# Full 128 rows in the bias product and in the transposes of a mixture-of-experts stage

## The chip, the core and the metric

The kernel runs on one core of one Trainium2 chip. The metric is the device time of one execution in microseconds (us), lower is better. On this kernel a measurement tells apart differences of about 0.2% (some 5 us). The engines are called as in the profile: PE is the tensor engine's products, PEld its loads of the stationary operand, DVE the vector engine, ACT the scalar engine, POOL GpSimd, SP the queue that issues most transfers.

## What is computed

One layer of a decoder on 1024 tokens of 1024 channels, in float32: two token mixers side by side, merged by gates, an output projection and a layer norm; then a mixture of 32 experts, of which each token takes 4, and a second layer norm. The change touches the experts alone. Cut to them, the reference is:

```
logits = (xt @ router_w + router_b); top_vals, top_idx = lax.top_k(logits, 4); gates = softmax(top_vals)
# for every expert e, over the tokens that chose it (xblk):
    hcat = xblk @ w_up[e] + b_up[e]                       # 1024 -> 2048
    x_glu = minimum(hcat[:, 0::2], 7); x_lin = clip(hcat[:, 1::2], -7, 7)
    act = x_glu * sigmoid(1.702 * x_glu) * (x_lin + 1)
    y = act @ w_down[e] + b_down[e]                       # 1024 -> 1024
# out[token] += gate * y
```

## The kernel before

Up to about 1040 us of its span the kernel does the mixers, the projections, the first layer norm and the router. The router writes, for each expert, a list of its tokens to DRAM, and sorts the experts by their counts. The experts then run from about 1045 to 2583 us, and a last layer norm ends the span.

**Two forms of an expert.** `CAPS` gives each place of the sorted order a fixed size n. The 18 largest experts have n from 204 down to 134 and are called *wide*: the weights are the stationary operand and the tokens stream past them. The other 14 have n = 128 and are *narrow*: the tokens are stationary and 512 columns of weights stream past. `SEQ` sets the order in which they run: mostly a wide and a narrow one in turn, and three times two wide ones in a row.

**Precision.** Each float32 operand is split in two parts whose sum it is (`split`: ACT makes the first part, DVE or, for every fifth piece of weights, POOL the second). A product of two split operands takes three products on PE. Weights arrive in transfers of 1 MB into six places (`raw`, `fetch`, issued by SP), are split six pieces of work ahead (`part`) into eight places each for `wh` and `wl`, and are then multiplied.

**Tokens of an expert.** `gather` (an indirect transfer on the POOL queue) brings the expert's tokens as rows into `xg`: block 0 with 128 tokens, and for a wide expert block 1 with the other n - 128, which are 76 for the first expert and 6 for the last wide one. `turn` transposes them on PE by way of the identity `idn`, 128 channels at a time, into a bank of PSUM (`tr`, two buffers), from where `split` makes the two parts in `xTA` (wide) or `xTB` (narrow). A transpose of block 1 works on as many rows as the block has tokens. One call of `turn` handles G channel blocks, as many as fit into 512 columns: 4 of a narrow expert, 3 or 2 of a wide one. So for a wide expert the PE sees an alternation of 128-row and short transposes, in groups of six or four. The groups of the next expert stand between the pieces of the one that runs.

**Biases.** A wide expert adds the bias of its first product while ACT evacuates it. A narrow expert adds it on PE: as the last product into each of its four accumulators (`up_narrow`, L1304), a column of the permutation `perm`, broadcast to 128 columns, is stationary and 512 columns of `bupr` stream past. Both have 64 rows: 32 experts' first parts and, below them, the 32 second parts.

**Order.** Each engine takes its instructions in the order in which the program writes them. `experts` writes it out by hand: a list of pieces (`order`), and beside it a list `side` of small jobs, of which one is called after a piece when nothing else is due. The turns of the next expert are such jobs; those that are left are called just before the next expert's first product.

Of the kernel before, what the change touches and what calls it, by code (L numbers as in the profile page):

```python
# [15 lines left out]
OP = mybir.AluOpType  # L16
# [53 lines left out]
def lockstep(*streams):  # L70
    """Emits generators side by side; each yields the tensor-engine time of the piece it emitted."""
    total = [0.0] * len(streams)
    live = set(range(len(streams)))
    weight = [w for _, w in streams]
    gens = [g for g, _ in streams]
    while live:
        i = min(live, key=lambda j: total[j] / weight[j])
        try:
            total[i] += next(gens[i])
        except StopIteration:  # L80
            live.discard(i)


def shape_constants():
    """Arrays of zeros and ones that hang on the shapes alone."""
# [29 lines left out]
class Block:  # L115
# [56 lines left out]
    def scratch(self):  # L172
        """Expert lists in DRAM: (token, gate) by expert and place; at first every place names a zero row."""
# [16 lines left out]
    def load_x(self):  # L190
        nc, a = self.nc, self.a
        # by half of the tokens
        self.xh = [p.tile([128, KT, 512], F32R, name=f"xh{i}") for i, p in enumerate(self.xpool)]
        self.xl = [p.tile([128, KT, 512], F32R, name=f"xl{i}") for i, p in enumerate(self.xpool)]
        # the place of q and f, which come later, takes the rows
# [21 lines left out]
    def fetch(self, col):  # L217
        """Loads columns col..col+256 of w_in and splits them."""
# [10 lines left out]
    def project(self, jobs, ahead=None):  # L229
        """jobs: (column, halves, evacuate): 256 columns by channel for these halves of the tokens, or by token for  # L230
        all of them where halves is None. A generator over pieces of tensor-engine work.

        ahead: a generator whose steps come before those of the first job.
        """
# [62 lines left out]
    def hgrn_jobs(self):  # L297
        """Projections of the HGRN branch: q^T and f^T by channel, v and the output gate by token."""
# [43 lines left out]
    def hgrn_chunks(self):  # L342
        """Chunks of 128 tokens: one chunk's decays beside the scores of the one before."""
# [17 lines left out]
    def hgrn_front(self, c, state):  # L361
        """Log gates of a chunk, their sums over ranges of tokens, and what these scale."""
# [15 lines left out]
        # q beside what the odd tokens' q keeps of the token before  # L378
# [10 lines left out]
        # decays from each token to the chunk's end  # L389
# [7 lines left out]
        for g, n in enumerate((4, 3)):  # L397
            for h in range(NH):
# [6 lines left out]
                for i in range(n):  # L405
# [5 lines left out]
                    # the first half of each block takes k, the second q  # L411
# [7 lines left out]
    def hgrn_back(self, c, state):  # L419
        """Scores within a chunk, its output, and the state it leaves."""  # L420
# [8 lines left out]
        # a token with itself and with the one before  # L429
# [52 lines left out]
    def rsqrt(self, pool, v, scale, eps, n):  # L482
        """1 / sqrt(v * scale + eps), with a Newton step on the table's value."""
# [14 lines left out]
    def sb_tiles(self):  # L498
        sp = self.spool
        # the first part of a head's keys lies on both halves of the partitions  # L500
        self.kh = sp.tile([128, SBH, T], F32R, name="kh")
        self.kl = sp.tile([128, 4, T], F32R, name="kl")
        self.sv = sp.tile([128, NB, 512], F32, name="sv")

    def sb_jobs(self):
        """q^T, kept in DRAM, k^T in two parts, v by token."""
# [33 lines left out]
    def gates_jobs(self):  # L540
        """The merge gates' arguments, by channel, kept in DRAM until the merge; a part of them early, a part late."""
# [15 lines left out]
    def sb_attention(self):  # L557
        """Weights sigmoid(z_s) * prod over s < s' < t of sigmoid(-z_s'), s < t."""
        nc, wk = self.nc, self.work
        self.os_d = self.dram("osb_scratch", (T, 512))  # L560
        # a unit is a head's block of queries, or several heads' where the keys are few
# [10 lines left out]
        def split_q(i):  # L572
            # the first part on the head's own partitions, the second on the others
# [8 lines left out]
        def heads(u):  # L582
            # those on the same half of the partitions follow one another: their products share a bank
# [4 lines left out]
        def scores(u):  # L588
# [28 lines left out]
            # a token keeps all of what itself and later ones would take  # L617
# [35 lines left out]
        def average(u):  # L653
            # two heads side by side, by channel
# [41 lines left out]
    def turn_branches(self):  # L696
        """The branches' outputs by channel, in two parts."""
# [4 lines left out]
        # the stick-breaking branch is there by channel: its own place in memory takes it  # L702
# [107 lines left out]
    def layer_norm(self, pool, r, st, g, b, out):  # L810
        """From the statistics of both halves of the rows."""
# [9 lines left out]
    def outproj(self):  # L821
# [6 lines left out]
        # the first part of the biases twice and the second, one below the other  # L828
# [3 lines left out]
        def load_biases(i):  # L832
            n = bd.shape[0] if i == 0 else self.bupr.shape[0]
# [5 lines left out]
        def round_biases(i):  # L839
            to = self.bupr[:, D * i - D:D * i] if i else bd  # L840
# [21 lines left out]
        def add(tb, half):  # L862
            """The residual, and the statistics of what results."""
# [5 lines left out]
        def project(tbs):  # L869
            """Blocks of tokens; two at a time follow the loading of the weights row block by row block."""  # L870
# [26 lines left out]
        def route(tb):  # L897
# [10 lines left out]
            # four sums side by side, by expert, then their sum by token  # L908
# [17 lines left out]
            # which experts each token takes, and with what weight  # L926
# [31 lines left out]
            # places within the experts' lists  # L958
# [26 lines left out]
            # what the experts' outputs are added to: the residual and the weighted biases  # L985
# [36 lines left out]
        # then the last block first: the order of the experts waits for it  # L1022
# [11 lines left out]
    def expert_constants(self):  # L1034
        """What the sorting needs, and the biases in two parts, the second below the first."""
# [13 lines left out]
        self.bupr = cp.tile([2 * NE, 2 * D], F32R, name="bupr")  # L1049

    def sort_experts(self):
        """Each expert's place in the order of the counts."""
# [4 lines left out]
        # distinct keys: the count, then the lower expert first  # L1057
# [19 lines left out]
        self.perm = cp.tile([2 * NE, NE], F32R, name="permr")  # L1077
# [3 lines left out]
    def sort_biases(self):  # L1081
        nc, cp = self.nc, self.epool
        # biases of the first product, by channel and place in the order
# [11 lines left out]
    def list_beyond(self):  # L1095
        """What lies beyond the static sizes: blocks of 128 places, listed."""
# [15 lines left out]
        # row of an expert's first block beyond, less 128 for each block listed before  # L1112
# [4 lines left out]
        # one block a partition: its expert and its first row  # L1117
# [15 lines left out]
        # the same along a row  # L1133
# [11 lines left out]
        self.itoh = cp.tile([2 * NE, NITEM], F32R, name="itoh")  # L1145
        nc.vector.tensor_scalar(self.itoh, ps[:2 * NE, :NITEM], self.ecol, None, op0=OP.is_equal)

    # Two forms of an expert's product. Up to 128 places: the tokens are the stationary operand and the
    # weights stream past. More: the weights are stationary and both parts of the tokens stream past them.

    def expert(self, n, e, rows, bias, choice):
# [11 lines left out]
        def gather():  # L1163
            ti = X["ti"]
            xg = wk.tile([128, 2, D], F32, name="xg", bufs=1)
# [6 lines left out]
        G = min(4, 512 // n)  # L1172

        def turn(k0):
# [5 lines left out]
            pv = ps[:, :(k1 - k0) * n].rearrange("p (k n) -> p k n", n=n)  # L1180
            for k in range(k0, k1):
                for i, (s, m) in enumerate(blocks):
                    nc.tensor.transpose(pv[:, k - k0, s:s + m], X["xg"][:m, i, 128 * k:128 * k + 128],
                                        self.idn[:m, :m])
# [567 lines left out]
```

## Time and profile before

| What | Before |
|---|---|
| Device time, median of 3 runs | 2642.2 us (2641.92 to 2643.72) |
| Profiled execution, span from the first to the last instruction | 2635.2 us |
| PE busy over the span | 2507.8 us (95%) |
| DVE, ACT, POOL busy | 1865.8, 1452.9, 866.9 us |
| Experts, first to last product | about 1056 to 2583 us |

The profile is of one execution; its span is 7.0 us shorter than the median time, and this part lies around the span. A busy time is a mean over stages with different limits, so what bounds a stage is read from its own stretch of the trace: from the waits of the engine that is nearly always busy there, and from the starts of its instructions. Products on PE are pipelined and overlap in the trace, so the distance from one start to the next tells their cost, and not the duration.

### The profile page before, as it was taken

Reading aid. Unit: us, or ns where it says so; the run is one execution under the profiler, and the core shown is the slowest. Engines: PE = TensorE matmul, PEld = TensorE weight load, DVE = VectorE, ACT = ScalarE, POOL = GpSimd, SP = SyncE. Lnnn points to the kernel's source line nnn. Section 1 sums busy time; section 2 is a strip of 40 time slices with the busy share of each in tenths; the row PEclk is TensorE's granted clock in tenths of the full one; section 3 lists DMA queues with packets and bytes.
Section 4 is the critical chain, followed back from the end, with each engine's and each line's share of the span. In section 5 each row is a group of like instructions: output and inputs, shape, how many; then the busy total and the mean of one; then the engine's idle time right before and its main releaser. Section 6 shows DMA issues by size and latency. Waiting matters only on the chain. (4 is left out here: it accounts for less than half of the span.)

```text
span 2635.2 us, 41833 instructions
## 1 busy us (share of the span) xinstructions
PE 2507.8 (95%) x15476; PEld 2180.4 (83%) x15476; DVE 1865.8 (71%) x3091; ACT 1452.9 (55%) x2499; POOL 866.9 (33%) x742
## 2 busy tenths in 40 slices
PE   8999999999989995999999999999999999999992
PEld 8898888887767763988988999889988899888982
DVE  3227674347784576777788788887888888888785
ACT  3213332235563311666676677776777767777772
POOL 1010110013121233443434354434544434444443
PEclk9999999999999997999999999999999999999996
DMA  5321323233124524898998889999899998999973
GB/s 163 95 81 52 94 91 104 68 80 89 49 81 145 158 93 154 273 304 271 297 285 282 267 271 305 297 296 282 266 301 297 309 287 280 308 306 307 316 216 137
DMA packets 426788, 550.57 MB, mean 209 GB/s; under 512 B 21382, under 2 KB 312342, under 8 KB 426580
## 3 DMA queue, kind: packets, MB, share of 16 engines
q1 hardware_dynamic: 403684, 476.76, 56.1%
q0 software_dynamic: 22608, 70.05, 9.3%
q8 instruction: 123, 2.02, 0.3%
q10 hardware_dynamic: 288, 1.05, 0.1%
q14 instruction: 85, 0.70, 0.1%
HBM read 496.33 MB, written 51.47 MB: 208 GB/s over the span
## 5 line engine op out<-in xcount | busy, mean ns | idle before, releaser
L126 DVE TENSOR_TENSOR wl<-raw,wh 128x1024 fp32r<-128x1024 f32 x671 | 886.2, 1335 | 205.6 <-ACT wh L125 201.9
L125 ACT CAST wh<-raw 128x1024 fp32r<-128x1024 f32 x824 | 843.9, 1047 | 67.9 <-PE pj L269 20.6
L1216 PE MATMUL mm<-xTA,wh 128*128 128x292 f32 (+16 forms) x2304 | 617.5, 355 | 0.0
L126 POOL TENSOR_TENSOR wl<-raw,wh 128x1024 fp32r<-128x1024 f32 x153 | 377.3, 2466 | 541.1 <-ACT wh L125 481.6
L1218 PE MATMUL mm<-xTA,wl 128*128 128x146 f32 (+16 forms) x2304 | 545.0, 237 | 0.0
L1218 PEld LDWEIGHTS mm<-xTA,wl 128*128 128x128 f32 x2304 | 455.1, 198 | 0.5
L1216 PEld LDWEIGHTS mm<-xTA,wh 128*128 128x128 f32 x2304 | 450.8, 196 | 3.6 <-issue 2.7
L1265 PE MATMUL mm<-aTA,wh 128*128 128x292 f32 (+16 forms) x1152 | 300.4, 347 | 1.6 <-POOL aTA L126 1.6
L1267 PE MATMUL mm<-aTA,wl 128*128 128x146 f32 (+16 forms) x1152 | 270.9, 235 | 0.0
L1265 PEld LDWEIGHTS mm<-aTA,wh 128*128 128x128 f32 x1152 | 216.5, 188 | 5.6 <-POOL aTA L126 2.0
L1267 PEld LDWEIGHTS mm<-aTA,wl 128*128 128x128 f32 x1152 | 220.1, 191 | 0.0
L130 PE MATMUL pj<-xh,wh 128*128 128x512 f32 x512 | 209.4, 409 | 0.0
L126 POOL TENSOR_TENSOR aTA<-gl,aTA 128x146 fp32r<-128x146 f32 (+16 forms) x144 | 114.6, 803 | 285.9 <-ACT aTA L125 277.5
L132 PE MATMUL pj<-xh,wl 128*128 128x512 f32 x512 | 201.1, 393 | 0.0
L131 PE MATMUL pj<-xl,wh 128*128 128x512 f32 x512 | 200.7, 392 | 0.0
L1299 PE MATMUL mm<-wh,xTB 128*128 128x512 f32 x448 | 188.4, 420 | 0.0
L1301 PE MATMUL mm<-wh,xTB 128*128 128x512 f32 x448 | 176.3, 394 | 0.0
L1300 PE MATMUL mm<-wl,xTB 128*128 128x512 f32 x448 | 175.4, 391 | 0.0
L1225 ACT ACTIVATE gl<-mm,bup 128x146 f32<-128x146 f32 (+16 forms) x288 | 97.2, 389 | 134.1 <-PE mm L1218 132.4
L1235 DVE TENSOR_TENSOR gl<-gl 128x146 f32<-128x146 f32 (+16 forms) x144 | 107.4, 746 | 11.1 <-ACT gl L1234 10.9
L132 PEld LDWEIGHTS pj<-xh,wl 128*128 128x128 f32 x512 | 96.7, 189 | 21.3
L130 PEld LDWEIGHTS pj<-xh,wh 128*128 128x128 f32 x512 | 96.8, 189 | 20.8 <-issue 2.5
(346 smaller groups left out, 4671.5 us busy)
## 6 DMA issues: line engine op xcount, KB each, us to landing
raw<-in_expert_w_up_dram SPq DMA_DIRECT2D x252, 1024.0 KB, 5.9
raw<-in_expert_w_down_dram SPq DMA_DIRECT2D x128, 1024.0 KB, 7.0
raw<-in_w_in_dram SPq DMA_DIRECT2D x56, 512.0 KB, 5.3
gate_scratch<-pe POOLq DMA_DIRECT2D x32, 256.0 KB, 2.3
gate<-gate_scratch SPq DMA_DIRECT2D x8, 1024.0 KB, 5.1
qf<-in_x_dram SPq DMA_DIRECT2D x8, 512.0 KB, 8.1
qraw<-q_scratch SPq DMA_DIRECT2D x16, 256.0 KB, 4.6
xt<-in_x_dram SPq DMA_DIRECT2D x8, 512.0 KB, 3.5
```

What stands on the lines that cost most here:

```text
L125: nc.scalar.copy(hi, src)
L126: (engine or nc.vector).tensor_tensor(lo, src, hi.bitcast(F32), op=OP.subtract)
L130: nc.tensor.matmul(ps, wh, xh, start=start, stop=False)
L131: nc.tensor.matmul(ps, wh, xl, start=False, stop=False)
L132: nc.tensor.matmul(ps, wl, xh, start=False, stop=stop)
L1216: nc.tensor.matmul(ps[g][:, :2 * n], wh[:, kk, g::2], x[:, k].rearrange("p a n -> p (a n)"), start=k == 0, stop=False)
L1218: nc.tensor.matmul(ps[g][:, :n], wl[:, kk, g::2], x[:, k, 0], start=False, stop=k == KT - 1)
L1265: nc.tensor.matmul(ps[i][:, :2 * n], wh[:, kk, s], act[:, k].rearrange("p a n -> p (a n)"), start=k == 0, stop=False)
L1267: nc.tensor.matmul(ps[i][:, :n], wl[:, kk, s], act[:, k, 0], start=False, stop=k == KT - 1)
L1299: nc.tensor.matmul(p, x[:, k, 0], wh[:, kk], start=k == 0, stop=False)
L1300: nc.tensor.matmul(p, x[:, k, 0], wl[:, kk], start=False, stop=False)
L1301: nc.tensor.matmul(p, x[:, k, 1], wh[:, kk], start=False, stop=False)
```

## The change

The bias product and the transposes of gathered tokens always use 128 rows. `bupr`, `perm` and the one-hot columns `itoh` (used only for what lies beyond the static sizes) get 128 partitions, with zeros in the upper 64. `xg` becomes one tile that lives through the whole stage; its block 1 is zeroed once, so that rows past an expert's tokens hold finite numbers. Each transpose takes 128 rows and 128 columns, and what `split` reads of it is cut back to n. A wide expert needs 256 columns of PSUM for each channel block then, so G is 2 for all wide experts (it was 3 for the 14 with n up to 168), and 4 for narrow ones as before. `xg` is allocated last in the stage's memory and not second, so that the tiles between move by its size. Comments were taken out of the source as well, which changes line numbers alone.

```diff
@@ expert_constants
-        self.bupr = cp.tile([2 * NE, 2 * D], F32R, name="bupr")
+        self.bupr = cp.tile([128, 2 * D], F32R, name="bupr")
+        nc.gpsimd.memset(self.bupr[2 * NE:].bitcast(F32), 0.0)
@@ sort_experts
-        self.perm = cp.tile([2 * NE, NE], F32R, name="permr")
+        self.perm = cp.tile([128, NE], F32R, name="permr")
+        nc.vector.memset(self.perm[2 * NE:].bitcast(F32), 0.0)
@@ list_beyond
-        self.itoh = cp.tile([2 * NE, NITEM], F32R, name="itoh")
-        nc.vector.tensor_scalar(self.itoh, ps[:2 * NE, :NITEM], self.ecol, None, op0=OP.is_equal)
+        self.itoh = cp.tile([128, NITEM], F32R, name="itoh")
+        nc.vector.memset(self.itoh[2 * NE:].bitcast(F32), 0.0)
+        nc.vector.tensor_scalar(self.itoh[:2 * NE], ps[:2 * NE, :NITEM], self.ecol, None, op0=OP.is_equal)
@@ expert: gather, turn
-            xg = wk.tile([128, 2, D], F32, name="xg", bufs=1)
+            xg = self.xg
...
-        G = min(4, 512 // n)
+        G = 4 // nb
...
-            pv = ps[:, :(k1 - k0) * n].rearrange("p (k n) -> p k n", n=n)
+            pv = ps.rearrange("p (k n) -> p k n", n=128 * nb)
             for k in range(k0, k1):
                 for i, (s, m) in enumerate(blocks):
-                    nc.tensor.transpose(pv[:, k - k0, s:s + m], X["xg"][:m, i, 128 * k:128 * k + 128],
-                                        self.idn[:m, :m])
-            self.split(x[:, k0:k1, 0], x[:, k0:k1, 1], pv)
+                    nc.tensor.transpose(pv[:, k - k0, s:s + 128], X["xg"][:, i, 128 * k:128 * k + 128], self.idn)
+            self.split(x[:, k0:k1, 0], x[:, k0:k1, 1], pv[:, :, :n])
@@ expert: up_narrow
-            nc.tensor.matmul(p, choice.to_broadcast([2 * NE, 128]), self.bupr[:, 512 * c:512 * c + 512],
+            nc.tensor.matmul(p, choice.to_broadcast([128, 128]), self.bupr[:, 512 * c:512 * c + 512],
                              start=False, stop=True)
@@ experts
-                ("raw", [128, 2048], F32, self.nraw), ("xg", [128, 2, D], F32, 1), ("yo", [128, 2, D], F32, 2),
+                ("raw", [128, 2048], F32, self.nraw), ("yo", [128, 2, D], F32, 2),
...
+        self.xg = self.work.tile([128, 2, D], F32, name="xg")
+        nc.gpsimd.memset(self.xg[:, 1], 0.0)
```

The first place is PE's order while a narrow expert runs its first product and the tokens of the next, wide expert (n = 158, 30 tokens in block 1) are turned. A row gives the line, the operation, output and inputs, and the size of the output. Before:

```order
L1301 MATMUL mm<-wh,xTB 128x512
L1304 MATMUL mm<-bupr,permr 128x512
L1183 MATMUL tr<-idn,xg 128x128
L1183 MATMUL tr<-idn,xg 128x30
L1183 MATMUL tr<-idn,xg 128x128
L1183 MATMUL tr<-idn,xg 128x30
L1183 MATMUL tr<-idn,xg 128x128
L1183 MATMUL tr<-idn,xg 128x30
L1299 MATMUL mm<-wh,xTB 128x512
L1300 MATMUL mm<-wl,xTB 128x512
```

and after the change (L1305 is the line L1301 of before, L1308 is L1304, L1188 is L1183, L1303 and L1304 are L1299 and L1300):

```order
L1305 MATMUL mm<-wh,xTB 128x512
L1308 MATMUL mm<-bupr,permr 128x512
L1188 MATMUL tr<-idn,xg 128x128 x4
L1303 MATMUL mm<-wh,xTB 128x512
L1304 MATMUL mm<-wl,xTB 128x512
```

The bias product (L1304, then L1308) stands where it stood; its rows of input are not in this view. A group has four equal transposes in place of six that alternate. The fourth turn, which this expert has anew, stands behind the narrow expert's last bias product, just before the first product of the wide one (lines L1220 and L1222 are L1216 and L1218 of before):

```order
L1305 MATMUL mm<-wh,xTB 128x512
L1308 MATMUL mm<-bupr,permr 128x512
L1188 MATMUL tr<-idn,xg 128x128 x4
L1220 MATMUL mm<-xTA,wh 128x316
L1222 MATMUL mm<-xTA,wl 128x158
```

The second place is POOL's order at the start of the stage, with the semaphores that each row waits for: the last two scatters of the token lists, then the first expert's gathers. Before:

```order
L972 DMA tab_scratch<-rows,idx 36864x2 [waits DMASW1_49]
L971 MEMSET spacer 1x1 [waits Pool_49]
L972 DMA tab_scratch<-rows,idx 36864x2 [waits DMASW2_49]
L1167 DMA xg<-h_scratch,ti 128x1024 [waits DMAHW1_49,DMAHW5_49,DMASW3_49,PE_49]
L1167 DMA xg<-h_scratch,ti 76x1024 [waits DMASW4_49]
```

and after the change:

```order
L972 DMA tab_scratch<-rows,idx 36864x2 [waits DMASW1_49]
L971 MEMSET spacer 1x1 [waits Pool_49]
L972 DMA tab_scratch<-rows,idx 36864x2 [waits DMASW2_49]
L1453 MEMSET xg 128x1024 [waits PE_49]
L1171 DMA xg<-h_scratch,ti 128x1024 [waits DMAHW5_49,DMAHW1_49,DMASW3_49]
L1171 DMA xg<-h_scratch,ti 76x1024 [waits DMASW4_49,Pool_49]
```

The new memset takes over the wait for PE that the first gather had.

## Rows read from the trace of the kernel before

**Rows 1.** The page, part 1: busy us (share of the span) xinstructions.

```profile
PE 2507.8 (95%) x15476; PEld 2180.4 (83%) x15476; DVE 1865.8 (71%) x3091; ACT 1452.9 (55%) x2499; POOL 866.9 (33%) x742
```

**Rows 2.** Waits of PE, 1045 to 2585 us: us in total, times, longest.

```profile
PE tr L1183 <- DMA xg<-h_scratch,ti: 16.0, 2, 10.7
PE tr L1323 <- DVE gl L1315: 3.2, 4, 2.1
```

**Rows 3.** Windows: length, then busy time by engine, granted clock, DMA share, GB/s.

```profile
core 0: us, PE busy (x) PEld busy (x) DVE busy (x) ACT busy (x) POOL busy (x), PEclk, DMA share, GB/s
...
2250.00:2520.00 270.00, 269.60 (x1746) 238.53 (x1745) 221.50 (x325) 198.72 (x323) 119.73 (x74) 1.00 0.96 305
...
sum 1521.00, PE 1514.21 PEld 1364.40 DVE 1240.21 ACT 1077.02 POOL 653.78; mean PE 151.42 PEld 136.44 DVE 124.02 ACT 107.70 POOL 65.38
```

**Rows 4.** Line 1304: duration ns min/median/max, first and last start, forms; idle before.

```profile
L1304 PEld LDWEIGHTS mm<-bupr,permr x56: 182/182/182, 1103.6 to 2519.3; 64*128 64x128 f32 x56
...
  issue: 20.2, 56
```

**Rows 5.** Timeline of PE around one bias product: start, duration, line, operation, shapes.

```profile
1103.31 0.39 PE L1301 MATMUL mm<-wh,xTB 128*128 128x512 f32 x1
1103.63 0.49 PE L1304 MATMUL mm<-bupr,permr 64*128 64x512 f32 x1
1104.05 0.45 PE L1265 MATMUL mm<-aTA,wh 128*128 128x408 f32 x1
1104.34 0.26 PE L1267 MATMUL mm<-aTA,wl 128*128 128x204 f32 x1
1104.43 0.37 PE L1265 MATMUL mm<-aTA,wh 128*128 128x408 f32 x1
1104.64 0.26 PE L1267 MATMUL mm<-aTA,wl 128*128 128x204 f32 x1
```

**Rows 6.** Timeline of PE, two turns of a wide expert with 20 tokens in block 1.

```profile
1917.08 0.39 PE L1300 MATMUL mm<-wl,xTB 128*128 128x512 f32 x1
1917.32 0.39 PE L1301 MATMUL mm<-wh,xTB 128*128 128x512 f32 x1
1917.54 1.28 PE L1183 MATMUL tr<-idn,xg 128*128 128x128 f32 x6
...
1919.09 0.40 PE L1300 MATMUL mm<-wl,xTB 128*128 128x512 f32 x1
...
1920.02 0.39 PE L1301 MATMUL mm<-wh,xTB 128*128 128x512 f32 x1
1920.25 0.86 PE L1183 MATMUL tr<-idn,xg 128*128 128x128 f32 x4
...
1921.37 0.40 PE L1300 MATMUL mm<-wl,xTB 128*128 128x512 f32 x1
```

**Rows 7.** Timeline of PE, four transposes of outputs, all with 128 rows (L1287).

```profile
1128.36 0.39 PE L1301 MATMUL mm<-wh,xTB 128*128 128x512 f32 x1
1128.59 0.60 PE L1287 MATMUL tr<-idn,yT 128*76 128x128 f32 x4
...
1129.26 0.39 PE L1300 MATMUL mm<-wl,xTB 128*128 128x512 f32 x1
```

**Rows 8.** Timeline of PE, the first expert's turns (76 tokens in block 1).

```profile
1053.22 1.41 PE L1183 MATMUL tr<-idn,xg 76*128 76x76 f32 x7 [5.23 <-DMA xg<-h_scratch,ti]
1055.16 1.63 PE L1183 MATMUL tr<-idn,xg 128*128 128x128 f32 x8 [0.53 <-DVE xTA L126]
```

**Rows 9.** POOL: a memset by line (us, mean ns); two waits, by timeline.

```profile
L184 POOL MEMSET E<- 128x512 f32 x1 | 0.5, 547 | 0.0
897.16 1.49 POOL L837 DMA_DIRECT2D ac<-in_expert_b_down_dram  x3 [2.04 <-DVE wol L126]
1040.40 1.02 POOL L1167 DMA_INDIRECT xg<-h_scratch,ti  x1 [8.04 <-DMA ti<-tab_scratch]
```

**Rows 10.** SP's waits, 2400 to 2520 us; ACT's, 1062 to 2583 us; one window.

```profile
SPq L1194 <- DVE wl L126: 56.3, 22, 4.6
ACT wh L125 <- DMA raw<-in_expert_w_up_dram: 11.2, 3, 7.7
1160.00:1180.00 20.00, 20.00 (x130) 19.26 (x129) 16.89 (x24) 13.78 (x24) 10.88 (x6) 1.00 1.06 338
```

More of the change, by code (lines that the diff above doesn't have):

```diff
@@ L832, in load_biases @@
         def load_biases(i):
-            n = bd.shape[0] if i == 0 else self.bupr.shape[0]
+            n = bd.shape[0] if i == 0 else 2 * NE
             raw[i] = wk.tile([128, D], F32, name="ac", bufs=2)[:n]
@@ L839, in round_biases @@
         def round_biases(i):
-            to = self.bupr[:, D * i - D:D * i] if i else bd
+            to = self.bupr[:2 * NE, D * i - D:D * i] if i else bd
             n = to.shape[0] - NE
@@ L1505, in beyond @@
             nc.vector.tensor_copy(it, self.items[:1, :, ds(i, 1)].rearrange("o a b -> o (a b)"))
-            ch = wk.tile([2 * NE, 1], F32R, name="ch")
+            ch = wk.tile([128, 1], F32R, name="ch")
             nc.vector.tensor_copy(ch, self.itoh[:, ds(i, 1)])
```

## The prediction

> **What bounds the kernel now.** I read the page first, then PE's waits in the experts, then windows, then the timeline of PE around the instructions that the change touches. PE is busy for 95% of the span [rows 1], but that is a mean, and a busy PE may still be waiting inside its pipeline. The change touches only the experts (1045 to 2583 us) and some constants before them. There PE waits for other engines for about 20 us in all: 16.0 us for the first expert's tokens, at the very start, and a few us later [rows 2]. From 1062 to 2583 us it is busy for 1514 of 1521 us, DVE for 1240, ACT for 1077 and POOL for 654, at a granted clock of 1.00, which is the 2.4 GHz level [rows 3]. So in this stage PE's own sequence sets the end, and each microsecond taken out of it shortens the kernel until another supplier is late. What the page can't show is how much of PE's sequence is stall. For that one looks at starts: in the trace PE's idle time before the loads of the bias product's stationary operand is put down to "issue", 20.2 us for 56 of them, 0.36 us each [rows 4]. No semaphore that the profile shows ended that wait.
>
> **The bias product.** In [rows 5] the product before it starts at 1103.31, the bias product at 1103.63, the next product at 1104.05 and the one after that at 1104.34. Products of 512 columns normally follow at 0.23 us (1917.08 to 1917.32 in [rows 6]), and a 408-column product is followed after 0.21 us (1104.43 to 1104.64 in [rows 5]). So the three steps take 1.03 us where 0.23 + 0.23 + 0.21 = 0.67 would do: 0.36 us too much, before and after the only product with 64 rows. That the columns are the same 512 speaks for the rows as the cause. With 128 rows I take the product at the pace of its neighbours. 14 narrow experts have 4 each: 56 x 0.36 = **20.2 us**. The bounds are 0 (the stall stays) and 20.2 us; I take the upper one, because the nearest rows, all other 128-row products, have no such stall.
>
> **The transposes of the tokens.** In [rows 6] six alternating transposes stand between products that start at 1917.32 and 1919.09: 1.77 us, less 0.46 for the two products, is 1.31 us of cost, and the group of four costs 1921.37 - 1920.02 - 0.46 = 0.89 us. This expert has 20 tokens in block 1, the middle of the 14 wide ones that turn in groups of six, six and four. With the three that turn in four groups of four, there are 28 sixes and 14 + 12 = 26 fours: 28 x 1.31 + 26 x 0.89 = 59.8 us. Afterwards there are 17 x 4 = 68 groups of four with 128 rows and 128 columns. That form is in the trace already: the transposes of a wide expert's outputs, at the same place between the same products, take 1129.26 - 1128.36 - 0.46 = 0.44 us [rows 7], a third of the group of six, though four times 128 are 512 columns and the six stream only 444. 68 x 0.44 = 29.9 us, so **29.9 us** less. Here too the lower bound is a loss, worked out as the fourth rival.
>
> The first expert is apart. Its block 1 has 76 tokens, over 64, and its transposes run at a slower pace, soon after PE has stood still for tokens. Eight of them go from 76 to 128 columns. If time goes by columns, eight transposes of which half are short take 1.63 us [rows 8], a full one 0.25, and eight more times 0.4 of it are 0.8 us. I take **0.8 us** as a loss, since this group lies on the path to the first product; the bound below is 0.
>
> Why rows should matter is not in the profile, which says "issue". The Trainium skill has a rule for it in TensorEngine Tiling (Array Packing), section Key Properties: a change of the tiling mode, not only of the tile, drains the engine, and its list of modes has 64 rows as one of the row tilings. By that rule the trace agrees: 0.36 us are lost around 64 rows [rows 4, 5] and nothing of the kind around 128 [rows 7].
>
> **What it adds.** (1) 11 wide experts that follow a narrow one get a fourth turn, which stands just before their own first product (the order above); the second piece of that product reads what it makes. The three experts that have four turns already do just this, and PE shows no wait for it [rows 2]. I take 0; the bound is 1 us each, 11 us, if the split is late by one cast. (2) 14 more splits on ACT and DVE, of smaller size: at most 0.6 us each on engines that have 444 and 281 us to spare [rows 3]; hidden. (3) POOL zeroes 64x2048 of `bupr` before the router. A 128x512 memset took 0.55 us [rows 9], so some 2.2 us by an estimate from that row. Behind it on POOL stand the loads of the router's weights and biases; the latter wait 2.04 us for DVE anyway [rows 9]. If the cover were gone they would come 2.2 us later, and they are needed some 30 us on. (4) POOL zeroes 128x1024 of `xg`, 1.1 us by the same row, ahead of the first gathers. They wait 8.04 us for the list of tokens [rows 9], and the memset stands in that wait. Uncovered it would cost 1.1 us, once. (5) Two small memsets on DVE, 0.2 us each, one in the sort of the experts, whose results are not what the first gather waits for last. (6) Tiles that lie 8 KB lower: the first casts wait for more of the previous stage's transfers. Weights are late there anyway, and I allow 1 us either way.
>
> **The sum.** 20.2 + 29.9 - 0.8 = 49.3 us. The profiled span goes from 2635.2 to about 2586 us, and with the 7.0 us around it the time goes from 2642.2 to **2593 us**.
>
> **Can the suppliers follow?** PE's pace rises by 3.3%. In the densest stretch, 2250 to 2520 us, DVE is at 221.5 of 270 us, so it would go from 82 to 85%; DMA's share is 0.96 at 305 GB/s [rows 3]. That looks full, but the share is no ceiling: 1160 to 1180 us shows 1.06 at 338 GB/s, and 305 x 1.033 is 315. SP's queue waits for a free place in `raw` (56.3 us of 120 for DVE alone), and ACT waited for weights only 3 times in the whole stage [rows 10]. Transfers wait for places and not the other way round.
>
> **The rivals.**
> *Full gain*, as summed: 2590 to 2598 us, chance 0.75.
> *The supply holds it back.* If DMA or DVE can't go faster from about 1950 us on, 570 of 1521 us gain nothing: 49.3 x 570/1521 = 18.5 us lost, 2611 us. For it speaks the share of 0.96, against it the 1.06 elsewhere. Chance 0.10.
> *A new wait.* The late fourth turn makes PE wait up to 1 us in 11 experts: 2604 us. Against it are the three experts without such a wait. Chance 0.07.
> *One half only.* The stall goes in the bias product but stays in the transposes' operands, or the reverse: gains of 19 or 29 us, 2613 to 2623 us. Chance 0.04.
> *Slower.* The stalls hang on something that the change keeps: the column broadcast to 128 for the bias product, or the change between two blocks of `xg`. Then only columns are added. The second blocks of 17 experts grow by 1734 columns in all, times 8 channel blocks; a group of 512 columns costs 0.44 us [rows 7], so 13872 columns are 11.9 us, and with 14 more groups at 0.1 us for the product behind each, and 0.8 us at the start, the kernel takes 14 us more: 2656 us. It decides as soon as less than a quarter of the stalls goes. Against it stand the narrow groups and [rows 7], where neither stall nor short rows are seen. Chance 0.03. A page speaks for this one: TensorE: Matmul & The Clock Gate of the Trainium skill, section LDWEIGHTS, says that a load of 32 rows takes as long as one of 128, since columns alone count. The loads' own durations agree (182 ns with 64 rows [rows 4]), the gaps between starts don't.
> *No change at all* (within 0.2%, 5 us, which is about what a measurement here can tell): only if gains and losses happened to cancel. Chance 0.01.
>
> **How the numbers follow.** The likeliest case gives 2593 us. Its own uncertainty is 2 us for the pace of the groups and 1 us at the start. The range goes up to 2608 so that it takes in the new wait and most of what a supplier could take back, and down to 2588 for stalls somewhat larger than in the sample rows. Faster by over 0.2%: 0.75 + 0.10 + 0.07 + 0.04 = 0.96; within: 0.01; slower: 0.03.
>
> **What would show it.** In the changed kernel's timeline the bias product should start 0.23 us after its neighbour and be followed at the same distance, with no "issue" idle at its line. A group of four of a wide expert should cost 0.44 us like [rows 7]. PE's waits should stay near the 20 us of now, and the span up to 1040 us should not move. I would be wrong if ACT's wait for weights or PE's wait for `xTA` grew to more than a few us, or if the starts around the bias product stayed at 0.32 and 0.42 us.

## The result, and the profile after

The changed kernel takes **2604.0 us** (median of 4 runs, 2603.6 to 2604.7) against 2642.8 (4 runs of the kernel before beside it): ratio 0.9855, 95% interval 0.9841 to 0.9869. It is 38.8 us faster, inside the range, but 10.5 us less than the 49.3 of the sum. The profiled execution has a span of 2602.2 us. Page, part 1, to be read beside [rows 1]:

```profile
PE 2464.0 (95%) x15476; PEld 2180.7 (84%) x15476; DVE 1870.6 (72%) x3107; ACT 1454.7 (56%) x2513; POOL 869.2 (33%) x744
```

First the pieces that the change touches, since they say whether the stalls went. Line 1308 is the bias product (L1304 in [rows 4]):

```profile
L1308 PEld LDWEIGHTS mm<-bupr,permr x56: 187/188/188, 1106.3 to 2486.1; 128*128 128x128 f32 x56
L1308 PE MATMUL mm<-bupr,permr x56: 390/394/402, 1106.6 to 2486.4; 128*128 128x512 f32 x56
its engine sat idle before it (us, times) until:
who waited for it (us, times):
```

Nothing stands under "sat idle", where before there were 20.2 us of "issue". PE's timeline around the same product as in [rows 5], and around one group of four transposes (L1188, L1183 before):

```profile
1106.34 0.39 PE L1305 MATMUL mm<-wh,xTB 128*128 128x512 f32 x1
1106.57 0.39 PE L1308 MATMUL mm<-bupr,permr 128*128 128x512 f32 x1
1106.80 0.34 PE L1269 MATMUL mm<-aTA,wh 128*128 128x408 f32 x1
...
1142.05 0.39 PE L1305 MATMUL mm<-wh,xTB 128*128 128x512 f32 x1
1142.28 0.60 PE L1188 MATMUL tr<-idn,xg 128*128 128x128 f32 x4
1142.64 0.48 PE L1303 MATMUL mm<-wh,xTB 128*128 128x512 f32 x1
1142.95 0.39 PE L1304 MATMUL mm<-wl,xTB 128*128 128x512 f32 x1
```

The bias product starts 0.23 us after its neighbour and is followed 0.23 us later. The group costs 1142.95 - 1142.05 - 0.46 = 0.44 us, as [rows 7] had it. Added up over all starts from 1062 us on, the time that all turns and bias products add between the products around them falls from 103.6 to 52.6 us: **51.0 us are gone**, where the first two terms of the sum had 50.1.

So the 10.5 us were lost elsewhere. PE's waits from 1045 to 2550 us (us in total, times, longest), beside [rows 2]:

```profile
PE tr L1188 <- DMA xg<-h_scratch,ti: 16.8, 2, 11.1
PE tr L1327 <- DVE gl L1319: 11.8, 11, 2.5
PE mm L1269 <- POOL aTA L126: 3.2, 4, 1.3
```

The wait for the tokens stays. The wait of the activations' transposes (L1327, L1323 before) for the last step of the narrow experts' gate on DVE (`gl`, L1319) is 11.8 us where it was 3.2, and a wait for `aTA` is 3.2 where the same answer of the kernel before had 0.4. The timeline of all engines shows one of the long ones, behind the last bias product of a narrow expert at 1754.57 (rows of other instructions left out; in brackets the idle time before and what ended it):

```profile
1754.80 0.60 PE L1188 MATMUL tr<-idn,xg 128*128 128x128 f32 x4
...
1757.17 0.42 ACT L1318 ACTIVATE gl<-gl 128x256 f32<-128x256 f32 x1 [0.37 <-DVE gl L1312]
1757.39 0.46 DVE L126 TENSOR_TENSOR xTA<-tr,xTA 128x308 fp32r<-128x308 f32 x1
1757.78 1.21 DVE L126 TENSOR_TENSOR wl<-raw,wh 128x1024 fp32r<-128x1024 f32 x1
1758.66 2.54 POOL L126 TENSOR_TENSOR wl<-raw,wh 128x1024 fp32r<-128x1024 f32 x1 [6.65 <-ACT wh L125]
1758.91 2.58 DVE L1319 SCALAR_TENSOR_TENSOR gl<-gl 128x256 f32<-128x256 f32 x1
1761.64 0.41 PE L1327 MATMUL tr<-idn,gl 128*128 128x128 f32 x2 [2.10 <-DVE gl L1319]
...
1762.57 0.63 PE L1342 MATMUL mm<-wh,aTB 128*128 128x512 f32 x1
1762.99 0.63 PE L1340 MATMUL mm<-wh,aTB 128*128 128x512 f32 x1
```

The four transposes at 1754.80 are the wide expert's fourth turn, which the change made. Its split on DVE (1757.39, 0.46 us) stands before the gate in DVE's queue. The gate begins at 1758.91, a quarter of a microsecond after a weight piece on POOL, and takes 2.58 us, ending 0.29 us after that piece. PE waits 2.10 us for it, and then its products follow at 0.42 us: the granted clock has fallen to the lower level, 1.2 GHz. In this profile three such waits of 2.1 us stand behind last gates where there was none before, and three of 0.3 to 0.4 us. Long gates as such are not new: by DVE's timeline the kernel before has 10 of over 1.7 us among its 56, and PE waited at most 0.4 us for one of them. The changed kernel has 13 of 2.35 to 2.81 us, and the three more are just these three last gates. Two stretches of 3.4 us at the lower clock follow (the kernel before had none in the experts); at half the pace they cost 1.7 us each.

This accounts for the experts: 51.0 - 8.6 (gate) - 2.8 (`aTA`) - 3.4 (clock) = 36.2 us. From the first bias product to the end of the span it is 2635.2 - 1103.6 = 1531.6 us before and 2602.2 - 1106.6 = 1495.6 after, **36.0 us** less.

### The profile page after: what moved, and what is told of

It is laid out like the page before. It is cut to its first block, busy times and chain, and to the rows that moved or that the text cites. A ratio compares the mean times of both kernels' runs of the same rounds, so it can differ in the third digit from the quotient of the medians.

```text
span 2602.2 us, 41853 instructions
## 1 busy us (share of the span) xinstructions
PE 2464.0 (95%) x15476; PEld 2180.7 (84%) x15476; DVE 1870.6 (72%) x3107; ACT 1454.7 (56%) x2513; POOL 869.2 (33%) x744
## 5 line engine op out<-in xcount | busy, mean ns | idle before, releaser
L1220 PE MATMUL mm<-xTA,wh 128*128 128x292 f32 (+16 forms) x2304 | 616.8, 355 | 0.0
L1222 PE MATMUL mm<-xTA,wl 128*128 128x146 f32 (+16 forms) x2304 | 544.6, 236 | 0.0
L1222 PEld LDWEIGHTS mm<-xTA,wl 128*128 128x128 f32 x2304 | 454.9, 197 | 0.5
L1220 PEld LDWEIGHTS mm<-xTA,wh 128*128 128x128 f32 x2304 | 450.4, 196 | 0.8
L1303 PE MATMUL mm<-wh,xTB 128*128 128x512 f32 x448 | 187.8, 419 | 0.0
L1305 PE MATMUL mm<-wh,xTB 128*128 128x512 f32 x448 | 176.3, 393 | 0.0
L1304 PE MATMUL mm<-wl,xTB 128*128 128x512 f32 x448 | 175.0, 391 | 0.0
L1239 DVE TENSOR_TENSOR gl<-gl 128x146 f32<-128x146 f32 (+16 forms) x144 | 113.6, 789 | 10.9 <-ACT gl L1238 10.7
```

Source lines behind the costliest of these rows:

```text
L1220: nc.tensor.matmul(ps[g][:, :2 * n], wh[:, kk, g::2], x[:, k].rearrange("p a n -> p (a n)"), start=k == 0, stop=False)
L1222: nc.tensor.matmul(ps[g][:, :n], wl[:, kk, g::2], x[:, k, 0], start=False, stop=k == KT - 1)
L1303: nc.tensor.matmul(p, x[:, k, 0], wh[:, kk], start=k == 0, stop=False)
L1304: nc.tensor.matmul(p, x[:, k, 0], wl[:, kk], start=False, stop=False)
L1305: nc.tensor.matmul(p, x[:, k, 1], wh[:, kk], start=False, stop=False)
```

## The experiments

Two questions: are rows the cause of the stalls, in both halves and for any number of rows (e1 to e3, e6), and what took 10.5 us back (e4, e5, e7 to e12): the fourth turn's own place, the wait for the gate, or the pieces on GpSimd that stand beside the gate. Ratios are against runs of the kernel before on the same chip (its medians there are 2640.1 to 2642.8 us). "Stage" is the time from the first bias product's start to the end of the span in the profiled execution; it leaves out what varies ahead of the experts. "Gate" is the sum of PE's waits for the last step of the gate (`gl`), in us. "Falls" counts the stretches at 1.2 GHz in the experts before 2520 us.

| kernel | median us | ratio (95%) | stage | gate | falls |
|---|---|---|---|---|---|
| before | 2642.8 | 1 | 1531.6 | 3.2 | 0 |
| changed | 2604.0 | 0.9855 (0.9841-0.9869) | 1495.6 | 11.8 | 2 |
| e1 bias product alone | 2623.1 | 0.9930 (0.9915-0.9945) | 1514.9 | 4.0 | 1 |
| e2 transposes alone | 2623.2 | 0.9928 (0.9913-0.9944) | 1513.1 | 9.7 | 2 |
| e3 bias with 96 rows | 2605.9 | 0.9867 (0.9852-0.9882) | 1495.7 | 12.1 | 1 |
| e4 turns one piece earlier | 2595.6 | 0.9826 (0.9813-0.9839) | 1487.0 | 3.7 | 1 |
| e5 activations one piece later | 2602.8 | 0.9846 (0.9833-0.9859) | 1494.3 | 8.6 | 3 |
| e6 second block with 68 rows | 2594.5 | 0.9812 (0.9798-0.9827) | 1484.9 | 6.2 | 1 |
| e7 = e6 and e4 | 2596.9 | 0.9830 (0.9817-0.9844) | 1486.0 | 8.6 | 0 |
| e8 = e6, e4 and e5 | 2600.3 | 0.9843 (0.9828-0.9857) | 1490.2 | 11.5 | 2 |
| e9 changed, no pieces on GpSimd | 2585.8 | 0.9790 (0.9774-0.9806) | 1478.3 | 0 | 0 |
| e10 = e6, no pieces on GpSimd | 2580.1 | 0.9772 (0.9756-0.9789) | 1472.6 | 0 | 0 |
| e11 before, no pieces on GpSimd | 2634.6 | 0.9983 (0.9973-0.9993) | 1526.4 | 0 | 0 |
| e12 = e7, no pieces on GpSimd | 2580.0 | 0.9766 (0.9749-0.9784) | 1472.7 | 0 | 0 |

**e1 and e2: one half each.** e1 has `turn` as before the change; e2 has the 64-row operands of the bias product (`bupr`, `permr`, `itoh`, `ch` and the broadcast) as before.

```diff
e1: -        G = 4 // nb
    +        G = min(4, 512 // n)
    -   nc.tensor.transpose(pv[:, k - k0, s:s + 128], X["xg"][:, i, 128 * k:128 * k + 128], self.idn)
    +   nc.tensor.transpose(pv[:, k - k0, s:s + m], X["xg"][:m, i, 128 * k:128 * k + 128], self.idn[:m, :m])
...
e2: -        self.bupr = cp.tile([128, 2 * D], F32R, name="bupr")
    +        self.bupr = cp.tile([2 * NE, 2 * D], F32R, name="bupr")
...
```

> Only the bias product has 128 rows; the transposes are as before (short rows, 3 or 2 channel blocks a turn). Theory A (a product with 64 rows costs 0.36 us more than a full one because of its rows): 56 x 0.36 = 20 us less, of which 0 to 2 us come back as waits for the gate of narrow experts: 2623 us (2621 to 2626), and no idle time put down to issue at the bias product. Rival B (the stall hangs on the broadcast operand): 2642 us.

> Only the transposes of tokens have 128 rows (and 2 channel blocks a turn for wide experts); the bias product keeps 64 rows. Theory A: the turns cost 30 us less, and the fourth turn of a wide expert, which stands after a narrow expert's last bias product, holds up that expert's last gate, so that some 8 to 10 us come back: 2622 us (2618 to 2626), with PE waits for gl at the transposes of the fourth chunk. Rival C (the waits come from the faster bias product): 2613 us, without these waits.

Each gives 19 us against the 2642.0 of the kernel before beside them. The bias term stands; the transposes bring 19 instead of 29, and the long waits for the gate come with them (9.7 us), not with the bias product (4.0). Both halves stall on their own, so "one half only" falls.

**e3: where the stall ends.** The bias product with 96 rows in place of 128, in all its operands.

```diff
-            nc.tensor.matmul(p, choice.to_broadcast([128, 128]), ...
+            nc.tensor.matmul(p, choice.to_broadcast([96, 128]), ...
...
```

> The changed kernel with the bias product at 96 rows instead of 128 (the zeros end at row 96). Theory A1 (the stall comes with at most 64 rows, as the first expert's 76-row transposes without one suggest): 2604 us, as the changed kernel. Rival A2 (any product with fewer than 128 rows stalls): 20 us more than the changed kernel, 2624 us.

PE's timeline around the first of them:

```profile
1105.88 0.39 PE L1305 MATMUL mm<-wh,xTB 128*128 128x512 f32 x1
1106.11 0.40 PE L1308 MATMUL mm<-bupr,permr 96*128 96x512 f32 x1
1106.35 0.35 PE L1269 MATMUL mm<-aTA,wh 128*128 128x408 f32 x1
```

96 rows run at the pace of 128, so it isn't fewer rows than the neighbours that stall, and the full 128 aren't needed.

**e4: the turns one piece earlier.** In the wide experts that follow a narrow one, so that the fourth turn no longer stands behind the last bias product.

```diff
-  if j == (15 if (CAPS[SEQ[q]] > 128) == (CAPS[SEQ[q + 1]] > 128) else 9):
+  if j == (15 if (CAPS[SEQ[q]] > 128) == (CAPS[SEQ[q + 1]] > 128) else 9 if CAPS[SEQ[q]] > 128 else 8):
```

> The changed kernel with the turns of a wide expert put into the list of side jobs one piece earlier while a narrow expert runs, so that all four are done before that expert's last bias product. Theory D (the missing 11 us of the changed kernel are the last gate of narrow experts, delayed by the split of the fourth turn: three waits of 2.1 us, three of about 0.35 us, and 1.7 us for each of two falls of the granted clock behind them): 2594 us (2592 to 2597), no wait for gl at the fourth chunk's transposes. Rival E (the waits come from POOL's pieces wherever they fall, and only move to other chunks): 2601 to 2605 us.

It takes 8.4 us off the changed kernel, as theory D had it: the loss hangs on the place of this turn. But at the spot shown above the gate was moved by only 0.39 us. Timeline, DVE and POOL:

```profile
1758.52 0.41 DVE L1319 SCALAR_TENSOR_TENSOR gl<-gl 128x256 f32<-128x256 f32 x1
1758.66 2.54 POOL L126 TENSOR_TENSOR wl<-raw,wh 128x1024 fp32r<-128x1024 f32 x1 [6.66 <-ACT wh L125]
```

It starts 0.14 us ahead of POOL's piece and takes 0.41 us. So it is a race by tenths of a microsecond, and the next runs asked whether POOL's piece is the cause.

**e5: the activations' transposes one piece later.**

```diff
-  [(1, gate_narrow, c), (3, turn_act, c)]
+  [(1, gate_narrow, c), (4, turn_act, c)]
```

> The changed kernel with one number more: the transposes of a narrow expert's activations come four pieces behind its last bias product in place of three, so TensorE asks for the gate's result some 2.3 us later; the early turns stay where the change put them. Theory W (the time that was lost in the experts is TensorE's wait for the gate, wherever the fourth turn stands): the 11.8 us of waits for VectorE's last gate step and the two short falls of the clock behind them go, nothing else moves: 2592 to 2596 us, and under 2 us of such waits left. Rival P (the fourth turn's place itself costs, by its split and its transposes; the wait is only where the profile shows it): the wait goes but another comes in its place: 2600 to 2604 us.

2602.8 us lies in the range of rival P, but P's mechanism isn't seen, and it was no clean test of W either. The waits of over 0.3 us at the first two gates of an expert went but for one of 0.45 us; those of 2.1 us at the last gate stayed: what an expert still owes is called before its own first down piece, so there the edit gave PE no later start, while the turns moved too. DVE and POOL at the same place, by the timeline:

```profile
1757.54 0.40 DVE L126 TENSOR_TENSOR aTB<-tr,aTB 128x256 fp32r<-128x256 f32 x1
1757.87 1.21 DVE L126 TENSOR_TENSOR wl<-raw,wh 128x1024 fp32r<-128x1024 f32 x1
1758.81 2.50 POOL L126 TENSOR_TENSOR wl<-raw,wh 128x1024 fp32r<-128x1024 f32 x1 [6.71 <-ACT wh L125]
1759.00 2.59 DVE L1319 SCALAR_TENSOR_TENSOR gl<-gl 128x256 f32<-128x256 f32 x1
```

A split of the activations (`aTB`, 0.40 us) now stands ahead of the gate in place of the turn's, and the gate again begins just behind POOL's piece, with 2.59 us. It needn't be the fourth turn's split.

**e6 to e8: a second block of 68 rows or more.**

```diff
-        G = 4 // nb
+        G = 4 if not wide else 3 if 2 * n + 128 + max(n - 128, 68) <= 512 else 2
-   nc.tensor.transpose(pv[:, k - k0, s:s + 128], X["xg"][:, i, 128 * k:128 * k + 128], self.idn)
+   r = max(m, 68)
+   o = (k - k0) * n + s
+   nc.tensor.transpose(ps[:, o:o + r], X["xg"][:r, i, 128 * k:128 * k + 128], self.idn[:r, :r])
```

> The second block of gathered tokens is transposed with its own tokens alone, but with 68 rows at least (7 of 8 of the 18 wide experts' second blocks have fewer): rows that never held a token are no longer streamed, and in 12 wide experts three turns (of 3, 3 and 2 blocks of columns) replace four. Theory S (a product of up to 64 rows stalls, one of 68 does not, as 96 did not): 8160 columns fewer behind the first expert at the 0.109 us that 128 of them take make 7.0 us, and the fourth turns that made TensorE wait at the gate are mostly gone, up to 8 us more: 2588 to 2597 us. Rival T (any transpose shorter than its 128-row neighbours stalls, as the 64-row ones did at about 0.1 us each way): 17 experts with 8 of them each, at 0.1 to 0.2 us, cost 14 to 27 us: 2604 to 2620 us.

> The kernel with 68 rows for the second block, and the turns queued one piece earlier in the wide experts that follow a narrow one. Theory S with the wait at the gate as the cause of what the change lost: 2604 less 7.0 for the columns less 8.4 for the waits: 2586 to 2591 us. Rival T: 2596 us or more.

> The same with the activations' transposes four pieces behind the bias product as well. If waits for the gate are all that is left of the loss: the 3.7 us of such waits that remain with the early turns go too: 2583 to 2588 us. If the waits left are only the profile's name for work that VectorE and GpSimd do beside each other, the time stays that of the kernel without this edit, within 1 us.

e6 came out in the range of theory S: six alternating transposes, half of them with 68 rows, by the timeline

```profile
1752.26 0.39 PE L1310 MATMUL mm<-bupr,permr 128*128 128x512 f32 x1
1752.49 0.68 PE L1190 MATMUL tr<-idn,xg 128*128 128x128 f32 x6
1752.98 0.47 PE L1305 MATMUL mm<-wh,xTB 128*128 128x512 f32 x1
1753.29 0.39 PE L1306 MATMUL mm<-wl,xTB 128*128 128x512 f32 x1
```

cost 1753.29 - 1752.26 - 0.46 = 0.57 us, where the six of before, with 20 rows in the short ones, cost 1.31 [rows 6]. The columns left out were worth less than its 7.0 us: by the starts, added up as above, 3.5 us between e9 and e10. e7 and e8 missed: the earlier turns brought nothing more and the later transposes cost 3 us. e7's 2596.9 us is what rival T named, but T's stall isn't there: its groups of six cost 0.57 us as well. In e7 new waits of 2.1 and 1.9 us stood behind third bias products, in e8 three of 2.3 to 2.4 us behind last ones. Each shift freed some gates and pushed others beside a piece of POOL's. Shifting the order was no cure.

**e9 to e12: no weight pieces on GpSimd.** VectorE computes each low part; nothing else changes.

```diff
-POOLED = 5
+POOLED = 100000
```

> The changed kernel, but every piece's low part is computed by VectorE; in the changed kernel each fifth (150 in the experts, 2.4 us each) was GpSimd's. Theory M (the gate's step, 0.41 us in 43 of 56 places, lasts 2.4 to 2.8 us in the other 13 because it starts beside such a piece of GpSimd): no gate step is above 0.6 us, and the waits of 2.1 us at the last gate of three narrow experts are under 0.5 us each. Of the time: 6 us of waits and 3 us of slower clock behind them could go, but VectorE takes 150 pieces of 1.22 us more, 182 us in some 1490, less what its own pieces no longer lose: 2595 to 2600 us if it keeps up, 2605 to 2625 us if it makes the splits late. Rival N (the 2.4 us are not GpSimd's doing): gate steps of 2.4 us and waits of 2 us remain in at least 5 places.

> The same in the kernel whose second blocks are transposed with 68 rows at least. Theory M: the gate's long steps and the 6.2 us of waits for them go: 2587 to 2592 us if VectorE keeps up; 2597 to 2615 us if it makes splits late. Rival N: long gate steps remain, 2593 us or more.

> The kernel before, but every piece's low part is computed by VectorE. Theory M (the change moved the gate of narrow experts to where GpSimd's pieces lengthen it, and lost there what it gained elsewhere): the kernel before had 3.2 us of waits for the gate and no fall of the clock in the experts, so little is won: 2634 to 2641 us, and the change is worth 49 to 55 us between this kernel and the changed one with the same edit (2585.8 us). Rival G (GpSimd's pieces cost either kernel the same, some 17 us, and the change brings 39 us with or without them): 2621 to 2627 us.

> The kernel with 68 rows for the second block and no pieces on GpSimd, with the turns queued one piece earlier in the wide experts that follow a narrow one as well. Theory M: with no long gate step there is no wait left that the earlier turns could remove: 2579 to 2582 us, that of the kernel without this edit (2580.05 us). Rival P (the fourth turn's place costs something of its own): 2572 to 2577 us.

The gate's step in the kernel before (L1315; us in total, mean ns), from a list of DVE's instructions:

```profile
L1315 DVE SCALAR_TENSOR_TENSOR gl<-gl 128x256 f32<-128x256 f32 x56 | 43.7, 780 | 5.5 <-ACT gl L1314 5.5
```

Gate step and splits on DVE by line and tile (ns min/median/max), in the changed kernel:

```profile
L1319 DVE SCALAR_TENSOR_TENSOR gl<-gl x56: 409/413/2814, 1114.3 to 2490.4; 128x256 f32<-128x256 f32 x56
L126 DVE TENSOR_TENSOR wl<-raw,wh x611: 1155/1216/4073, 1062.7 to 2534.5; 128x1024 fp32r<-128x1024 f32 x153
L126 DVE TENSOR_TENSOR aTB<-tr,aTB x56: 406/411/426, 1117.5 to 2492.7; 128x256 fp32r<-128x256 f32 x56
```

and in e9:

```profile
L1319 DVE SCALAR_TENSOR_TENSOR gl<-gl x56: 406/415/422, 1110.4 to 2471.2; 128x256 f32<-128x256 f32 x56
L126 DVE TENSOR_TENSOR wl<-raw,wh x764: 1203/1224/1524, 1062.9 to 2515.2; 128x1024 fp32r<-128x1024 f32 x191
```

Without POOL's pieces no gate takes over 0.42 us. In the changed kernel 13 of 56 took 2.35 to 2.81 us, each of them beside such a piece (11 began up to 0.32 us behind its start, two 0.10 us ahead of it), and the other 43, of which none began beside one, took 0.41. PE's waits in e9, from 1045 to 2540 us:

```profile
PE tr L1188 <- DMA xg<-h_scratch,ti: 17.1, 2, 11.2
...
PE mm L1269 <- POOL aTA L126: 1.2, 3, 0.7
```

No wait for the gate is left, and no fall of the clock in the experts. Against the changed kernel 11.8 + (3.2 - 1.2) + 3.4 = 17.2 us should go; the stage is 1495.6 - 1478.3 = 17.3 us shorter and the median 18.2. Theory M is shown for the gate and its waits; its time was underrated, here (2595 to 2600 us) and in e10 (2587 to 2592 us, against 2580.1).

e11 is the control: the kernel before wins only 5.4 us by the same edit. Between e11 and e9, where no gate is lengthened, the change is worth 2634.6 - 2585.8 = **48.8 us** (51 by the two ratios). The sum forecast 49.3. Between these two the stage shortens by 48.1 us, of the 51.0 that the starts give there too, and 1.2 of the rest are waits for `aTA`: so what the late fourth turn costs by itself is under 2 us. In e10 and e12 the earlier turns make no difference, 2580.1 and 2580.0 us; that says little of this turn, since only four last bias products of e10 have a turn behind them, three of them in the kernel before too. These two are the fastest kernels here, 60 us under the one before.

## Why the prediction was right, and where it was off

The measured 2604 us lies outside the 2590 to 2598 us of the likeliest case. It is in the range because that was drawn out to 2608 us for a new wait and a late supplier; a wait is what came, by another way than the one described.

**What bounds the kernel: right.** PE's own sequence set the end, and each stall removed there shortened the experts until a wait came.

**The bias product, 20.2 us: right.** e1 gives 18.9 us by the medians, with 1.7 us of slower clock and 0.8 us more waits for the gate in its profile, and the starts are at the forecast 0.23 us.

**The transposes, 29.9 us: right in the instructions, and part of it lost again.** Each group costs the 0.44 us of [rows 7]; e2 gives 18.8 us in all, with 6.5 us more waits for the gate and two falls of the clock (3.4 us).

**Rows as the cause: shown.** 128 and 96 rows run at the neighbours' pace and 68 nearly so (0.57 us for 588 columns, where 512 of the full form take 0.44); 64 [rows 5] and 20 [rows 6] don't. Between 64 and 68 nothing was tried. The rule of the Trainium skill that the prediction named (TensorEngine Tiling (Array Packing), Key Properties) fits this: 64 rows and 32 are among its row tilings, 96 and 68 are not. That a change of mode is what costs the time here is not shown. The rival "slower" falls.

**The first expert, 0.8 us: half of it.** PE's timeline of before, where the first product follows on the rows of [rows 8], and after the change:

```profile
1056.52 0.69 PE L1216 MATMUL mm<-xTA,wh 128*128 128x408 f32 x1
```

```profile
1056.23 1.73 PE L1188 MATMUL tr<-idn,xg 128*128 128x128 f32 x7 [5.62 <-DMA xg<-h_scratch,ti]
1058.31 1.97 PE L1188 MATMUL tr<-idn,xg 128*128 128x128 f32 x8 [0.35 <-DVE xTA L126]
1059.93 0.69 PE L1220 MATMUL mm<-xTA,wh 128*128 128x408 f32 x1
```

From the first of these transposes to the first product it is 3.70 us against 3.30, so 0.40 us are lost: each of the two groups takes over 0.3 us more, and the wait between them is 0.18 us shorter. From the issue of the load of the list of tokens to the first product it is 19.70 us against 18.75, but the rest of this difference is the arrival of the tokens, ahead of the transposes. That the span up to 1040 us would not move held but for some 2 us: the list landed 2.5 us later in the profiled execution, with two more falls of the clock ahead of the experts.

**The memsets, hidden: right.** By line (us, mean ns), POOL:

```profile
L1051 POOL MEMSET bupr<- 64x2048 f32 x1 | 1.8, 1815 | 0.0
L1453 POOL MEMSET xg<- 128x1024 f32 x1 | 1.0, 977 | 0.0
```

The estimates were 2.2 and 1.1 us. The second lies in the wait for the list of tokens.

**The suppliers follow: right**, and "the supply holds it back" falls: e10 is 60 us shorter than the kernel before, with DVE carrying all pieces.

**The failed step is added cost (1)**, the late fourth turn of 11 wide experts taken as 0, with (2), the splits called hidden. The reason was that three experts with four turns showed no wait. That was looked for at one place, PE's wait for `xTA`, and there it holds still. What was not asked is what the split is queued in front of: on DVE it goes ahead of the narrow expert's gate, and PE waits for that some 5 us behind the bias product. e2 and e4 show the loss at this place, e9 and e11 its mechanism. "Hidden" was read off the 281 us that DVE has to spare, a mean, where an order within tenths of a microsecond decided. The rival "a new wait" (2604 us, 0.07) was the right family and by chance the right time; its place (`xTA`) and its bound of 1 us each were not. Three waits were 2.1 us, because the gate meets a POOL piece of 2.4 to 2.5 us, and a slower clock followed two of them.

That [rows 2] already had 3.2 us of waits for this gate, one of 2.1, was read as "a few us later" and not followed. The trace of before had the mechanism: the gate's step took 780 ns in the mean (the row of L1315 above) where most take 0.41 us. And the wait of 2.1 us stood behind a gate of 0.42 us that was late itself: ahead of it on DVE a step on 64 numbers (L1130) took 3.03 us beside a piece of POOL's. In e11, without such pieces, it takes 0.15 us.

The profiled execution of before was quicker than its median: it was counted with 7.0 us around the span, while runs have about 1.6. The span's own gain (33.0 us) is therefore smaller than that of the medians (38.8), and the stage's (36.0) lies between.

## What to carry to other kernels

An inserted step costs where it is queued, so follow its instructions on every engine to what stands right behind them and to who waits for that; spare time in a mean doesn't hide it. When an instruction of fixed shape shows two durations, as the gate's 0.41 and 2.6 us, look for what starts just before the long ones. And when a change gives less than its instructions say, take the suspected interference away in both kernels: the pair tells what the change itself is worth.

## What the runs showed of the hardware

**GpSimd's help was worth nothing to VectorE.** Windows over the experts, the changed kernel and then e9 (length; busy time and count of PE, PEld, DVE, ACT, POOL; clock; DMA share, GB/s):

```profile
1062.00:2550.00 1488.00, 1471.33 (x9770) 1366.61 (x9769) 1247.65 (x1819) 1079.35 (x1792) 655.83 (x415) 1.00 0.91 293
```

```profile
1062.00:2532.00 1470.00, 1465.72 (x9774) 1364.63 (x9772) 1255.48 (x1973) 1075.54 (x1793) 244.46 (x260) 1.00 0.92 296
```

POOL gives up 411 us of work, and DVE, with 154 instructions more, is busy 8 us longer. At 1.22 us each they are 188 us, so it had lost some 180 us in waiting beside POOL. Only some forms wait. The gate's step and the `wl` splits, which take both inputs from SBUF, reach 2.8 and 4.1 us; the `aTB` split, with one input in PSUM, never passes 0.43, though 16 of its 56 began beside such a piece. The Trainium skill says this in SBUF — State Buffer, section Who interferes with whom: a VectorE instruction with two SBUF inputs contends with a GpSimd instruction that reads SBUF, and the order of issue decides which of the two is blocked. The trace agrees: the gate of 2.58 us ended 0.29 us after the piece beside which it began. In the records the order is blurred by about 0.1 us: the two gates that began 0.10 us ahead of a piece were held up like the others, the one of e4, 0.14 us ahead, was not. Two inputs are not the only case: the wide experts' clamp (L1231, TENSOR_SCALAR, one input, in SBUF) reached 2.54 us in the changed kernel and 0.55 in e9.

**The clock after a wait.** In the ten kernels with pieces on GpSimd, the one before among them, PE had 25 gaps of 2 us or more between two starts from 1064 to 2520 us. 13 of them were followed within 1.5 us by 3.4 us at the lower level, 1.2 GHz, and no such stretch began elsewhere there. What decides between the 13 and the other 12 was not tried. With the gaps gone (e9 to e12) there was none.
